# Reading bank Y on the scalar engine one product earlier, and reordering the first Strassen-like pair of each FFN

## The chip, the cores and the metric

One NeuronCore of a Trainium2 chip runs the whole kernel. The metric is the device time of one execution in microseconds. Three runs of the kernel before lie between 2317.99 and 2319.35 us, with a median of 2318.83 us. Engine names are those of the profile: PE (matrix multiply; its weight loads are PEld), DVE (vector), ACT (scalar), POOL (GpSimd) and SP (which issues the DMAs).

## What is computed

The reference is one encoder layer for 1280 tokens of width 1024 in float32: a SwiGLU half-step, a mixing step, and a second SwiGLU half-step. Only the FFNs matter here:

```python
def _swiglu(x, w_gate, w_up, w_down):
    return (jax.nn.silu(x @ w_gate) * (x @ w_up)) @ w_down

h = x + 0.5 * _swiglu(_rmsnorm(x, ffn1_norm), ffn1_w_gate, ffn1_w_up, ffn1_w_down)
...                                       # attention, retention, w_out
h = h + 0.5 * _swiglu(_rmsnorm(h, ffn2_norm), ffn2_w_gate, ffn2_w_up, ffn2_w_down)
return _rmsnorm(h, final_norm)
```

The FFN is 2816 wide, which is 22 blocks of 128 columns, taken two at a time as 11 pairs.

## The kernel before

**Precision.** Every float32 operand is split into a high half (an ACT cast, tiles `wh`, `xh`) and a low half (a DVE subtraction, `wl`, `xl`). A product is three matmuls: high by high, low by high, high by low. The page's names `pa` (a PSUM bank), `wh`, `wl`, `xh`, `xl` are these.

**FFN.** The 1280 tokens stand in three chunks: two of 512 columns and one of 256. Pair 0 of an FFN is multiplied directly (`direct`). Pairs 1 to 10 go through `seven_eighths`: the 1024 tokens of the two wide chunks are multiplied with seven products in place of eight (a Strassen-like scheme), once for gate and once for up (`product`, m = 0 and 1). The products carry numbers: 1, 2, 6, 7, 5, 4, 3, in this order, with 21 for a block that only the 256-column chunk needs. `seven` makes the weight factors (sums `s1` to `s4` on DVE, then the two halves of each). `combos` makes the activation factors of 6, 7, 5 and 4 on DVE. A product here is 12 matmuls of 128x512.

**Banks.** One `product` has five of the eight PSUM banks. X takes product 1, and later 6, 5 and 3 are added on top; Z takes product 2; Y takes product 7, and 4 is added on top. d1 and d2 hold the 256-column chunk, with 24 matmuls of 128x256 each. Outputs are read off between products: `o11` = X after 1 plus Z, `o21` = -X after 6, minus Y after 4. `o22` needs X after product 5 and Y after product 7:

```python
o22 = s2(name="o22")
nc.scalar.activation(o22, X, AF.Copy, scale=-1.0)
nc.vector.tensor_tensor(o22, o22, Y, op=ALU.subtract)
```

Product 4 is added on Y, so its first matmul waits until that DVE subtraction has read Y.

**Order.** `Weaver` records every instruction and then lists them for each engine by a planner with costs of its own, so that the program of an engine is a fixed list which the engine runs in order. All rows of the trace carry the line of `emit` (L433). Buffers of 128x512 come from one heap of 104 slots; a buffer gets a slot in the order in which the planner allocates.

**Before and after the FFN.** In `Lead`, the factors of the tokens are split; in the second FFN they come from the output projection (`out_unit`), whose last eight calls make chunk 2. Numbers at the end of a tile's name in the rows below only tell tiles apart.

Of the kernel before, what the change touches and what calls it, by code (L numbers as in the profile page):

```python
# [70 lines left out]
class Buf:  # L71
    def __init__(self, pool, shape, dt, tag, name, bufs, psum=False):
        self.args = (pool, shape, dt, tag, name, bufs)
        self.shape, self.tag, self.bufs, self.psum = shape, tag, bufs, psum
        self.width = shape[1]
        self.order = None
        self.left = 0
        self.end = 0.0
        self.accesses = []
        self.tile = None  # L80
# [19 lines left out]
class Weaver:  # L100
# [75 lines left out]
    def record(self, calls):  # L176
# [3 lines left out]
        for eng, method, a, k in calls:  # L180
            vals = [v for v in list(a) + list(k.values()) if isinstance(v, View)]
            outs = [k["out"]] if "out" in k else [a[0]]
            if k.get("accum_out") is not None:
                outs.append(k["accum_out"])
            outs = [v for v in outs if isinstance(v, View)]
            ins = [v for v in vals if not any(v is x for x in outs)]
            if method == "dma_start":
                v = (outs + ins)[0]
                nb = (v.box[1] - v.box[0]) * (v.box[3] - v.box[2]) * 4
                op.cost, op.lat, op.kind = 0.47, 2.0, nb  # L190
            else:
                op.cost += self.cost(eng, method, a, k, outs, ins)
                f = a[2] if method == "activation" and len(a) > 2 else None
                if f in (AF.Silu, AF.Exp):
                    op.kind = f
            for views, wr in ((ins, False), (outs, True)):
                for v in views:
                    b = v.buf
                    box = (0, P, 0, b.width) if b.psum else v.box
                    keep = []  # L200
                    for x in b.accesses:
                        (p0, p1, c0, c1), i, w = x

# [63 lines left out]
    def arrange(self, prio):  # L267
# [28 lines left out]
        self.peak = {n: max(t["seq"]) for n, t in self.tags.items()}  # L296

        def fresh(op):
            return [b for b in op.bufs.values() if b.tag is not None and not self.tags[b.tag]["done"][b.order]]

        def may(op):
            if op.eng == "SP" and op.idx > front() + self.AHEAD:
# [143 lines left out]
def tile_encoder_layer(ctx: ExitStack, tc: tile.TileContext, xT, wf1, w_in, w_out, wf2,  # L446
# [20 lines left out]
    def s2(dt=F32, name="t"):  # L467
        return nc.tile(hp, [P, 512], dt, "s2", nm(name), NS2)

    def two(W, name):  # L470

        if W <= 256:
            t = s2(F32R, name)
            return t[:, :W], t[:, 256:256 + W]
        return s2(F32R, name + "h"), s2(F32R, name + "l")

    def bank_a():
        return nc.tile(psp, [P, 512], F32, "p", nm("pa"), 8, True)
# [30 lines left out]
        nc.sync.dma_start(t, src)  # L509
        return t  # L510

    def halves(t, W=512):
        hi, lo = two(W, "w")
        split(t, hi, lo)
        return hi, lo

# [96 lines left out]
    def seven(r11, r12, r21, r22, W):  # L613
# [6 lines left out]
        yield 1, halves(r11, W)  # L620
        yield 2, halves(r12, W)
        nc.vector.tensor_tensor(s1, r21, r22, op=ALU.add)
        nc.vector.tensor_tensor(s2_, s1, r11, op=ALU.add)
        yield 6, halves(s2_, W)
        nc.vector.tensor_tensor(s3, r11, r21, op=ALU.add)
        yield 7, halves(s3, W)
        yield 5, halves(s1, W)
        yield 4, halves(r22, W)
        yield 21, halves(r21, W)
        nc.vector.tensor_tensor(s4, s2_, r12, op=ALU.add)  # L630
        yield 3, halves(s4, W)

    def norm_out(h, gcol, W, c0):
        pb = rms_rows(h, W)
        yield
        for kt in range(KT):
# [2 lines left out]
                                           op0=ALU.mult, op1=ALU.mult)  # L639
            nc.sync.dma_start(outT[:, kt, c0:c0 + W], t[:, :W])  # L640
            yield

    def ffn(tag, wsrc, leads, factors, load, after, direct_pairs):

# [7 lines left out]
        def product(t, m, hook):  # L652
# [49 lines left out]

        def direct(t, lead):

            ws, out, acts = {}, {}, {}

            def products(c):
                W = CH[c][1]
# [7 lines left out]
                for js in ((0, 1), (2, 3)) if c == 2 else ((0, 1, 2, 3),):  # L716
                    for k in range(2):
                        if k not in x:
                            x[k] = lead.x(c, k)
                        for j in js:  # L720
                            if (j, k) not in ws:
                                src = wsrc[t + j % 2 * HALF, :, j // 2, :]
                                ws[j, k] = halves(fetch(src[:, k * 512:(k + 1) * 512]))
                            part(out[c][j], ws[j, k], x[k], W, k == 0, k == 1)

            def close(c):
# [13 lines left out]
            close(1)  # L740
            return [acts[0][0], acts[1][0], acts[0][1], acts[1][1], *acts[2]]

        def seven_eighths(t, hook=lambda i: None):
            r = last.rows(2)
            acts = []
            for x in product(t, 0, lambda i: None):
                W = 512 if len(acts) < 4 else 256
                acts.append(gate(x, W, r if W < 512 else None))
            for i, x in enumerate(product(t, 1, hook)):
                W = 512 if i < 4 else 256  # L750
                up(acts[i], x, W, r if W < 512 else None)
            return acts
# [108 lines left out]
                first.update({j: [act(0, j)] for j in (1, 2, 6, 7, 5, 4, 3, 8, 9)})  # L861

        for t in range(direct_pairs, HALF):
            finish(t, seven_eighths(t, *[early] * (t == HALF - 1)))
        for c in range(3):
            h[c] = [None] * KT
        groups = [[0], [1, 2], [3, 4], [5, 6], [7, 8]]
# [54 lines left out]
    class Lead:  # L922


        def __init__(self, pairs, r2=None):
            self.pairs, self.r2 = pairs, r2

        def x(self, c, k):
            return self.pairs[c][4 * k:4 * k + 4]
# [7 lines left out]
    class First(Lead):  # L937


        def __init__(self):  # L940
            self.raw, self.pairs, self.r, self.n = {}, {0: [], 2: []}, {}, {}

        def x(self, c, k):
            if c != 1:
# [334 lines left out]
    for d in range(KT):  # L1279
        out_unit(1, d, cat[1])  # L1280
        if d == 3:
            cat[2] = cat_split(2)
    nx, xp = [], []
    for d in range(KT):
        out_unit(2, d, cat[2])
        if d in (0, 4):
# [11 lines left out]
        return t  # L1298

    def leads2():  # L1300
        yield Lead({0: xp[0], 1: xp[1], 2: x2})
        yield Lead({0: xp[0], 1: xp[1], 2: x2})

    def after2(c):
# [97 lines left out]
```

## Time and profile before

| | |
|---|---|
| median of 3 runs | 2318.83 us |
| the profiled execution, its own time | 2319.39 us |
| its span, first to last instruction | 2317.5 us |
| PE busy | 2270.6 us (98%) |
| DVE busy | 1589.7 us (69%) |
| ACT busy | 970.6 us (42%) |
| mean granted TensorE clock | 0.995 |

The span is 1.9 us shorter than the execution's time. PE is busy 98% of the span, and its idle time is the difference of 46.9 us. Which waits make it up stands in the view of waits; where they stand in time, in the timeline; what the clock did, in the view by windows. "pa <- DVE o" reads: a matmul into a bank `pa` was released by a DVE instruction that wrote `o`.

### The profile page before, as it was taken

What the parts mean: (1) busy time and instruction counts of PE and PEld (TensorE: products, weight loads), DVE (VectorE), ACT (ScalarE), POOL (GpSimd) and SP (SyncE); (2) the same over time, 40 slices, a digit from 0 to 9 for tenths busy, and PEclk for the clock granted to TensorE, in tenths of its full rate; (3) what the DMA queues carried; (4) which work ended last, traced back from release to release, by engine and by line L of the source; (5) the groups of instructions that cost most, each with busy time, mean ns of one, the idle gap of its engine ahead of it and who ended that gap; (6) DMA issues with size and microseconds to landing.
All of it is one profiled execution on the core that took longest, in us unless ns stands there. A gap on an engine that the chain in (4) does not pass through costs nothing.

```text
span 2317.5 us, 34127 instructions
## 1 busy us (share of the span) xinstructions
PE 2270.6 (98%) x12354; PEld 1937.2 (84%) x12354; DVE 1589.7 (69%) x3171; ACT 970.6 (42%) x2034; POOL 26.8 (1%) x31
## 2 busy tenths in 40 slices
PE   9999999999999999999999999989999999999998
PEld 8788888888888888887879979878888888888887
DVE  7966666556778876546778787666655555777866
ACT  7533443425422345234778474334333333432311
POOL 0000000000000000000000000000000000000000
PEclk9999999999999999999999999999999999999999
DMA  4333433345776643221134443234333334757722
GB/s 165 124 118 141 143 130 109 109 151 180 257 256 216 213 141 138 82 73 42 33 97 156 136 155 114 75 112 147 127 110 109 127 109 168 262 183 268 251 86 91
DMA packets 193417, 330.63 MB, mean 143 GB/s; under 512 B 20704, under 2 KB 45152, under 8 KB 193248
## 3 DMA queue, kind: packets, MB, share of 16 engines
q1 hardware_dynamic: 193248, 328.45, 41.0%
q8 instruction: 97, 1.59, 0.3%
q14 instruction: 72, 0.59, 0.1%
HBM read 226.65 MB, written 101.71 MB: 142 GB/s over the span
## 4 chain that ended last, share of the span: by engine, by line
PE 89%; DVE 5%; DMA 4%; issue 1%; ACT 1%; SPq 0%; POOL 0%; POOLq 0%; DVEq 0%; ACTq 0%
PE pa L433 63%; PE pb L433 25%; PE pc L433 2%; DMA raw<-wf 1%; DMA xa<-a 1%; DVE s L433 1%; DVE wl L433 1%; DVE h L433 1%; DMA h<-xT 1%; DVE o L433 1%; DVE xl L433 0%; DVE w L433 0%; DMA raw<-w_in 0%; DVE t L433 0%; SPq L433 0%
## 5 line engine op out<-in xcount | busy, mean ns | idle before, releaser
L433 PE MATMUL pa<-xh,wh 128*128 128x512 f32 x1664 | 659.9, 397 | 19.3 <-DVE o L433 15.3
L433 PE MATMUL pa<-xh,wl 128*128 128x512 f32 x1664 | 649.8, 390 | 8.0 <-DVE wl L433 8.0
L433 PE MATMUL pa<-xl,wh 128*128 128x512 f32 x1664 | 651.4, 391 | 1.0 <-DVE xl L433 1.0
L433 PE MATMUL pb<-xa,w 128*128 128x512 f32 (+1 forms) x2376 | 453.5, 352 | 6.0 <-ACT h L433 3.4
L433 PEld LDWEIGHTS pb<-xa,w 128*128 128x128 f32 x2376 | 386.4, 189 | 73.2 <-DVE h L433 6.3
L433 PEld LDWEIGHTS pa<-xh,wh 128*128 128x128 f32 x1664 | 314.0, 189 | 87.2 <-DVE o L433 19.1
L433 PEld LDWEIGHTS pa<-xh,wl 128*128 128x128 f32 x1664 | 313.5, 188 | 75.7 <-DVE wl L433 8.4
L433 PEld LDWEIGHTS pa<-xl,wh 128*128 128x128 f32 x1664 | 314.2, 189 | 58.7 <-DVE xl L433 1.8
L433 PE MATMUL pa<-x,wh 128*128 128x256 f32 x1824 | 337.5, 284 | 0.0
L433 PEld LDWEIGHTS pa<-x,wh 128*128 128x128 f32 x1824 | 294.9, 191 | 12.3
L433 DVE TENSOR_TENSOR wl<-raw,wh 128x512 fp32r<-128x512 f32 x372 | 244.4, 686 | 76.3 <-PE pa L433 38.6
L433 DVE SCALAR_TENSOR_TENSOR h<-pb,h 128x512 f32<-128x512 f32 (+1 forms) x360 | 223.4, 629 | 84.8 <-PE pb L433 81.9
L433 ACT CAST wh<-raw 128x512 fp32r<-128x512 f32 x372 | 217.2, 621 | 112.9 <-PE pa L433 49.8
L433 PE MATMUL pa<-x,wl 128*128 128x256 f32 x912 | 258.6, 284 | 0.1
L433 DVE TENSOR_TENSOR o<-o,pa 128x512 f32<-128x512 f32 x120 | 82.2, 685 | 179.6 <-PE pa L433 108.4
L433 ACT ACTIVATE o<-pa 128x512 f32<-128x512 f32 (+1 forms) x92 | 54.4, 591 | 312.6 <-PE pa L433 312.4
L433 PEld LDWEIGHTS pa<-x,wl 128*128 128x128 f32 x912 | 174.6, 191 | 0.4 <-DVE wl L433 0.3
L433 DVE TENSOR_TENSOR wl<-s,wh 128x512 fp32r<-128x512 f32 x160 | 106.9, 687 | 76.8 <-PE pa L433 64.0
L433 ACT CAST wh<-s 128x512 fp32r<-128x512 f32 x160 | 96.8, 619 | 34.4 <-PE pa L433 15.8
L433 ACT CAST w<-raw 128x256 fp32r<-128x256 f32 x144 | 53.7, 405 | 129.9 <-PE pb L433 97.8
L433 DVE TENSOR_TENSOR s<-s,raw 128x512 f32<-128x512 f32 (+1 forms) x152 | 85.2, 561 | 30.5 <-PE pa L433 28.5
L433 ACT CAST w<-s 128x256 fp32r<-128x256 f32 x144 | 56.0, 406 | 118.3 <-DVE s L433 68.1
(152 smaller groups left out, 2343.5 us busy)
## 6 DMA issues: line engine op xcount, KB each, us to landing
xa<-a SPq DMA_DIRECT2D x328, 256.0 KB, 5.1
raw<-wf SPq DMA_DIRECT2D x264, 256.0 KB, 4.3
a<-xh SPq DMA_DIRECT2D x142, 256.0 KB, 2.1
a<-xl SPq DMA_DIRECT2D x142, 256.0 KB, 3.3
raw<-w_in SPq DMA_DIRECT2D x132, 256.0 KB, 3.4
raw<-w_out SPq DMA_DIRECT2D x48, 256.0 KB, 3.1
a<-x SPq DMA_DIRECT2D x44, 256.0 KB, 2.5
h<-xT SPq DMA_DIRECT2D x32, 256.0 KB, 5.6
```

Of the source, the lines that this page charges most:

```text
L433: i = getattr(getattr(self.nc, eng), method)(*[r(x) for x in a], **{m: r(x) for m, x in k.items()})
```

## The change

Four things change.

- **Y is read first.** ACT reads Y as `o22` = -Y right after product 7, and DVE subtracts X after product 5. Product 4 may write to Y once ACT has read it, and product 3 may write to X once DVE has.
- **The first pair.** In the first pair that goes through `seven_eighths`, gate's products 1 and 2 are recorded, then up's products 1 and 2, then the rest of gate and the rest of up.
- **Slots.** In that pair the high and the low tile of a weight factor get their slots in one step (`mate`).
- **Weights ahead.** The eight weight blocks of the second FFN's pair 0 are fetched and split (`block`) ahead of the last eight calls of `out_unit`.

```diff
@@ Weaver.call
-                            b.order = len(t["bufs"])
-                            t["bufs"].append(b)
-                            op.allocs.append(b)
+                            for x in (b, b.mate) if b.mate is not None else (b,):
+                                x.order = len(t["bufs"])
+                                t["bufs"].append(x)
+                                op.allocs.append(x)
@@ two
-        return s2(F32R, name + "h"), s2(F32R, name + "l")
+        a, b = s2(F32R, name + "h"), s2(F32R, name + "l")
+        if together:
+            a.buf.mate, b.buf.mate = b.buf, a.buf
+        return a, b
@@ ffn
+    def block(wsrc, t, j, k):
+        return halves(fetch(wsrc[t + j % 2 * (NFF // 2), :, j // 2, k * 512:(k + 1) * 512]))
@@ product
-            for i, w in seven(*r, 512):
+            for i, w in seven(*r, 512, t == direct_pairs):
...
                 elif i == 7:
                     part(Y, w, xs[7], 512, True, True)
+                    o22 = s2(name="o22")
+                    nc.scalar.activation(o22, Y, AF.Copy, scale=-1.0)
                 elif i == 5:
                     part(X, w, xs[5], 512, False, True)
-                    o22 = s2(name="o22")
-                    nc.scalar.activation(o22, X, AF.Copy, scale=-1.0)
-                    nc.vector.tensor_tensor(o22, o22, Y, op=ALU.subtract)
+                    nc.vector.tensor_tensor(o22, o22, X, op=ALU.subtract)
...
                 hook(i)
-            return [o11, X, o21, o22, d1, d2]
+                if i == 2:
+                    yield
+            yield [o11, X, o21, o22, d1, d2]
@@ seven_eighths
-            for x in product(t, 0, lambda i: None):
+            ps = [product(t, 0, lambda i: None), product(t, 1, hook)]
+            next(ps[0])
+            if wait:
+                next(ps[1])
+            for x in next(ps[0]):
                 W = 512 if len(acts) < 4 else 256
                 acts.append(gate(x, W, r if W < 512 else None))
-            for i, x in enumerate(product(t, 1, hook)):
+            if not wait:
+                next(ps[1])
+            for i, x in enumerate(next(ps[1])):
@@ second FFN
+    ahead = {(j, k): block(wf2, 0, j, k) for j in range(4) for k in range(2)}
     for d in range(KT):
         out_unit(2, d, cat[2])
```

Three places of the engines' lists show what moves. The rows stand as each list has them, before and after apart.

PE in a pair of the second FFN, before: the last matmuls of d2 (`pa_3706`) and the first of product 4 on Y (`pa_3703`), which stands behind all of product 5's and 18 of d2's matmuls.

```order
L433 MATMUL pa_3706_17386<-x_3305_15321,wh_3726_16814 128x256 x2
L433 MATMUL pa_3706_17386<-x_3305_15321,wl_3727_17335 128x256 [waits DVE_49]
L433 MATMUL pa_3706_17386<-x_3307_15326,wh_3726_16814 128x256 x2
L433 MATMUL pa_3706_17386<-x_3307_15326,wl_3727_17335 128x256
L433 MATMUL pa_3703_17347<-xh_3390_15400,wh_3724_16808 128x512 [waits DVE_49]
L433 MATMUL pa_3703_17347<-xl_3391_15430,wh_3724_16808 128x512
```

After, product 4 on Y (`pa_3703`) follows product 5 on X (`pa_3702`) at once, and d2 comes behind it.

```order
L438 MATMUL pa_3702_17198<-xl_3425_15913,wh_3722_17270 128x512
L438 MATMUL pa_3702_17198<-xh_3424_15877,wl_3723_17312 128x512
L438 MATMUL pa_3703_17347<-xh_3390_15535,wh_3724_16808 128x512 [waits Activation_49]
L438 MATMUL pa_3703_17347<-xl_3391_15584,wh_3724_16808 128x512
L438 MATMUL pa_3703_17347<-xh_3390_15535,wl_3725_17333 128x512 [waits DVE_49]
```

Product 4's wait is now for ACT; all 24 matmuls of d2 stand behind product 4 and ahead of product 3.

DVE at the same place, before: five instructions, then the subtraction of Y from `o22`.

```order
L433 TENSOR_TENSOR wl_3763_17398<-raw_3739_16844,wh_3762_16974 128x512 [waits PE_49]
L433 TENSOR_TENSOR wl_3765_17400<-raw_3738_16827,wh_3764_16990 128x512 [waits PE_49]
L433 TENSOR_TENSOR s4_3748_17402<-s2_3746_17392,raw_3737_16819 128x512 [waits DVE_49]
L433 TENSOR_TENSOR wl_3802_17407<-raw_3788_17073,wh_3801_17272 128x512 [waits DVE_49]
L433 TENSOR_TENSOR o22_3723_17390<-o22_3723_17390,pa_3703_17347 128x512 [waits Activation_49]
```

After: the subtraction reads X (`pa_3702`), and the one of `o21` follows it.

```order
L438 TENSOR_TENSOR s3_3747_17377<-raw_3736_16769,raw_3738_16827 128x512
L438 TENSOR_TENSOR wl_3763_17384<-raw_3739_16844,wh_3762_16929 128x512 [waits PE_49]
L438 TENSOR_TENSOR wl_3755_17388<-s2_3746_17375,wh_3754_17379 128x512 [waits PE_49,Activation_49]
L438 TENSOR_TENSOR wl_3758_17401<-s3_3747_17377,wh_3757_17386 128x512 [waits Activation_49]
L438 TENSOR_TENSOR o22_3721_17369<-o22_3721_17369,pa_3702_17198 128x512 [waits PE_49]
L438 TENSOR_TENSOR o21_3718_17351<-o21_3718_17351,pa_3703_17347 128x512 [waits PE_49]
```

In each list some splits of the next factors stand ahead of the subtraction.

The second FFN's first pair on DVE, before: the low half of gate's plain factor 2 (`wl_3445`) stands behind the last combinations of the activations.

```order
L433 TENSOR_TENSOR xl_3421_15819<-n2_3417_15801,xh_3420_15809 128x512 [waits DMAHW3_49,Activation_49]
L433 TENSOR_TENSOR xl_3423_15823<-t3_3418_15807,xh_3422_15815 128x512 [waits DMAHW4_49,Activation_49]
L433 TENSOR_TENSOR xl_3425_15827<-t1_3416_15793,xh_3424_15803 128x512 [waits DMAHW5_49]
L433 TENSOR_TENSOR xl_3427_15831<-t4_3419_15813,xh_3426_15821 128x512 [waits Activation_49]
L433 TENSOR_TENSOR wl_3445_15833<-raw_3429_15115,wh_3444_15207 128x512 [waits DMAHW7_49]
```

After, it stands some sixty rows further ahead (row 2116 in place of 2179), together with that of up's factor 1 (`wl_3460`).

```order
L438 SCALAR_TENSOR_TENSOR n2_3381_15289<-t1_3380_15284,xn_3276_15164 128x512 [waits DVE_49]
L438 TENSOR_SCALAR r_3326_15300<-pb_3325_15293 128x2 [waits PE_49]
L438 TENSOR_TENSOR t3_3382_15302<-xn_3276_15164,xn_3272_15116 128x512
L438 SCALAR_TENSOR_TENSOR t4_3383_15310<-n2_3381_15289,xn_3213_14943 128x512 [waits DVE_49]
L438 TENSOR_TENSOR wl_3445_15315<-raw_3429_15118,wh_3444_15218 128x512 [waits DMAHW1_49]
L438 TENSOR_TENSOR wl_3460_15319<-raw_3446_15144,wh_3459_15222 128x512 [waits DMAHW4_49]
```

On PE the plain products of gate and of up and part of d2 now stand ahead of product 6 (`pa_3432` with `wh_3464`); these are the last rows ahead of it.

```order
L438 MATMUL pa_3454_15977<-x_3341_15391,wh_3492_15251 128x256 x2
L438 MATMUL pa_3454_15977<-x_3341_15391,wl_3493_15427 128x256
L438 MATMUL pa_3432_15706<-xh_3384_15304,wh_3464_15966 128x512 [waits Activation_49]
L438 MATMUL pa_3432_15706<-xl_3385_15510,wh_3464_15966 128x512
L438 MATMUL pa_3432_15706<-xh_3384_15304,wl_3465_15981 128x512 [waits DVE_49]
```

In the first FFN's first pair, PE before: product 6 (`pa_245`) and product 7 (`pa_246`) of the gate go one fourth at a time, as the activations come.

```order
L433 MATMUL pa_245_959<-xh_197_966,wh_259_517 128x512 [waits Activation_49]
L433 MATMUL pa_245_959<-xl_198_1066,wh_259_517 128x512 [waits DVE_49]
L433 MATMUL pa_245_959<-xh_197_966,wl_260_526 128x512
L433 MATMUL pa_246_1086<-xh_199_1061,wh_262_524 128x512 [waits Activation_49]
L433 MATMUL pa_246_1086<-xl_200_1073,wh_262_524 128x512 [waits DVE_49]
L433 MATMUL pa_246_1086<-xh_199_1061,wl_263_531 128x512
L433 MATMUL pa_285_1092<-xh_163_846,wh_295_606 128x512
```

After, up's product 6 (`pa_263`) takes part, and both plain products of up are done before.

```order
L438 MATMUL pa_245_987<-xh_197_992,wh_277_517 128x512 [waits Activation_49]
L438 MATMUL pa_245_987<-xl_198_1076,wh_277_517 128x512 [waits DVE_49]
L438 MATMUL pa_245_987<-xh_197_992,wl_278_526 128x512
L438 MATMUL pa_246_1119<-xh_199_1071,wh_280_524 128x512 [waits Activation_49]
L438 MATMUL pa_246_1119<-xl_200_1083,wh_280_524 128x512 [waits DVE_49]
L438 MATMUL pa_246_1119<-xh_199_1071,wl_281_531 128x512
L438 MATMUL pa_249_736<-x_11_128,wh_287_483 128x256 x2
L438 MATMUL pa_249_736<-x_11_128,wl_288_558 128x256
L438 MATMUL pa_263_1056<-xh_197_992,wh_297_581 128x512 [waits Activation_49]
L438 MATMUL pa_263_1056<-xl_198_1076,wh_297_581 128x512
```

The twelve matmuls of up's product 6 now stand among the fourths of gate's 6 and 7, three to each; up's product 2 (`pa_285`), which stood there before, has moved ahead of them, and three of d1's matmuls stand there in place of nine.

## Rows read from the trace of the kernel before

**Rows 1.** The page, part 1: busy time, share and instructions of each engine.

```profile
PE 2270.6 (98%) x12354; PEld 1937.2 (84%) x12354; DVE 1589.7 (69%) x3171; ACT 970.6 (42%) x2034; POOL 26.8 (1%) x31
```

**Rows 2.** The waits of PE, whole span: us in total, times, longest us.

```profile
PE pa L433 <- DVE o L433: 15.3, 17, 1.4
PE pa L433 <- DVE wl L433: 8.0, 1, 8.0
PE pa L433 <- ACT xh L433: 4.0, 2, 2.4
```

**Rows 3.** The waits of PE, 140 to 510 us (the first FFN).

```profile
PE pa L433 <- DVE o L433: 8.0, 8, 1.4
```

**Rows 4.** The waits of PE, 1525 to 2015 us (the second FFN).

```profile
PE pa L433 <- DVE o L433: 7.3, 9, 0.8
```

**Rows 5.** Timeline of PE, a pair of the second FFN: start, duration, instruction, [idle before].

```profile
1682.31 0.40 PE L433 MATMUL pa<-x,wh 128*128 128x256 f32 x2
1682.55 0.28 PE L433 MATMUL pa<-x,wl 128*128 128x256 f32 x1
1683.64 0.50 PE L433 MATMUL pa<-xh,wh 128*128 128x512 f32 x1 [0.81 <-DVE o L433]
1683.98 0.39 PE L433 MATMUL pa<-xl,wh 128*128 128x512 f32 x1
1684.21 0.40 PE L433 MATMUL pa<-xh,wl 128*128 128x512 f32 x1
```

**Rows 6.** Timeline of DVE around the same place.

```profile
1680.49 1.29 DVE L433 TENSOR_TENSOR wl<-raw,wh 128x512 fp32r<-128x512 f32 x2 [0.83 <-PE pa L433]
...
1682.91 0.68 DVE L433 TENSOR_TENSOR o<-o,pa 128x512 f32<-128x512 f32 x1
```

**Rows 7.** Timeline of DVE, a pair of the first FFN.

```profile
297.53 0.69 DVE L433 TENSOR_TENSOR wl<-raw,wh 128x512 fp32r<-128x512 f32 x1 [0.82 <-PE pa L433]
...
300.14 0.68 DVE L433 TENSOR_TENSOR o<-o,pa 128x512 f32<-128x512 f32 x1
```

**Rows 8.** Timeline of ACT, the same pair of the second FFN.

```profile
1680.72 0.60 ACT L433 ACTIVATE o<-pa 128x512 f32<-128x512 f32 x1 [3.08 <-PE pa L433]
1681.22 1.82 ACT L433 CAST wh<-s 128x512 fp32r<-128x512 f32 x3
```

**Rows 9.** Timeline of PE, where the casts of 1681.22 are first used.

```profile
1698.30 0.40 PE L433 MATMUL pa<-xh,wh 128*128 128x512 f32 x1
```

**Rows 10.** Windows: length, busy of PE, PEld, DVE, ACT, POOL, clock, DMA share, GB/s.

```profile
36.00:48.00 12.00, 12.00 (x71) 10.92 (x70) 7.43 (x16) 6.11 (x11) 2.99 (x3) 0.86 0.01 2
...
92.00:100.00 8.00, 3.32 (x10) 1.55 (x9) 7.93 (x14) 4.42 (x8) 0.00 (x0) 0.88 0.00 1
100.00:104.00 4.00, 3.64 (x9) 2.78 (x9) 4.00 (x9) 2.78 (x6) 0.00 (x0) 0.50 0.00 0
...
300.00:304.00 4.00, 3.12 (x15) 2.62 (x16) 1.04 (x3) 0.68 (x2) 0.00 (x0) 1.00 0.00 0
...
1506.00:1514.00 8.00, 0.27 (x2) 0.00 (x0) 7.97 (x14) 3.95 (x8) 0.00 (x0) 0.83 0.99 328
1514.00:1518.00 4.00, 3.74 (x9) 2.97 (x10) 2.80 (x6) 3.39 (x7) 0.00 (x0) 0.50 0.58 210
```

**Rows 11.** Timeline of PE, first pair of Strassen products in the second FFN.

```profile
1505.87 0.40 PE L433 MATMUL pa<-xl,wh 128*128 128x512 f32 x1
1514.26 0.80 PE L433 MATMUL pa<-xh,wl 128*128 128x512 f32 x1 [7.99 <-DVE wl L433]
```

**Rows 12.** Timeline of DVE, the same stretch.

```profile
1499.04 0.69 DVE L433 TENSOR_TENSOR s<-s,pa 128x512 f32<-128x512 f32 x1 [13.87 <-PE pa L433]
...
1513.52 0.68 DVE L433 TENSOR_TENSOR wl<-raw,wh 128x512 fp32r<-128x512 f32 x1
```

**Rows 13.** Timeline of PE, first pair of Strassen products in the first FFN.

```profile
94.36 0.49 PE L433 MATMUL pa<-xh,wh 128*128 128x512 f32 x1 [1.67 <-ACT xh L433]
...
99.30 0.80 PE L433 MATMUL pa<-xh,wh 128*128 128x512 f32 x1 [2.35 <-ACT xh L433]
```

More of the change, by code (lines that the diff above doesn't have):

```diff
@@ L75, in __init__ @@
         self.width = shape[1]
-        self.order = None
+        self.order = self.mate = None
         self.left = 0
@@ L298, in fresh @@
         def fresh(op):
-            return [b for b in op.bufs.values() if b.tag is not None and not self.tags[b.tag]["done"][b.order]]
+            new = [b for b in op.bufs.values() if b.tag is not None and not self.tags[b.tag]["done"][b.order]]
+            for b in list(new):
+                if b.mate is not None and not self.tags[b.tag]["done"][b.mate.order] and b.mate not in new:
+                    new.append(b.mate)
+            return new
         def may(op):
@@ L468, in s2, with two @@
         return nc.tile(hp, [P, 512], dt, "s2", nm(name), NS2)
-    def two(W, name):
+    def two(W, name, together=False):
         if W <= 256:
@@ L510, in fetch, with halves @@
         return t
-    def halves(t, W=512):
-        hi, lo = two(W, "w")
+    def halves(t, W=512, together=False):
+        hi, lo = two(W, "w", together)
         split(t, hi, lo)
@@ L611, in combos, with seven @@
         return {i: pair(t, 512) for i, t in ((6, n2), (7, t3), (5, t1), (4, t4))}
-    def seven(r11, r12, r21, r22, W):
+    def seven(r11, r12, r21, r22, W, together=False):
         if W > 256:
@@ L619, in seven @@
             s1, s2_, s3, s4 = a[:, :W], a[:, W:2 * W], b[:, :W], b[:, W:2 * W]
-        yield 1, halves(r11, W)
-        yield 2, halves(r12, W)
+        yield 1, halves(r11, W, together)
+        yield 2, halves(r12, W, together)
         nc.vector.tensor_tensor(s1, r21, r22, op=ALU.add)
         nc.vector.tensor_tensor(s2_, s1, r11, op=ALU.add)
-        yield 6, halves(s2_, W)
+        yield 6, halves(s2_, W, together)
         nc.vector.tensor_tensor(s3, r11, r21, op=ALU.add)
[L626 to L629, printed above, removed]
+        yield 7, halves(s3, W, together)
+        yield 5, halves(s1, W, together)
+        yield 4, halves(r22, W, together)
+        yield 21, halves(r21, W, together)
         nc.vector.tensor_tensor(s4, s2_, r12, op=ALU.add)
-        yield 3, halves(s4, W)
+        yield 3, halves(s4, W, together)
     def norm_out(h, gcol, W, c0):
@@ L703, in direct @@
         def direct(t, lead):
-            ws, out, acts = {}, {}, {}
+            ws, out, acts = lead.ws, {}, {}
             def products(c):
@@ L721, in products @@
                             if (j, k) not in ws:
-                                src = wsrc[t + j % 2 * HALF, :, j // 2, :]
-                                ws[j, k] = halves(fetch(src[:, k * 512:(k + 1) * 512]))
+                                ws[j, k] = block(wsrc, t, j, k)
                             part(out[c][j], ws[j, k], x[k], W, k == 0, k == 1)
@@ L741, in direct, with seven_eighths @@
             return [acts[0][0], acts[1][0], acts[0][1], acts[1][1], *acts[2]]
-        def seven_eighths(t, hook=lambda i: None):
+        def seven_eighths(t, wait, hook=lambda i: None):
             r = last.rows(2)
             acts = []
-            for x in product(t, 0, lambda i: None):
+            ps = [product(t, 0, lambda i: None), product(t, 1, hook)]
[3 more added lines that the diff above has]
+            for x in next(ps[0]):
                 W = 512 if len(acts) < 4 else 256
                 acts.append(gate(x, W, r if W < 512 else None))
-            for i, x in enumerate(product(t, 1, hook)):
+            if not wait:
+                next(ps[1])
+            for i, x in enumerate(next(ps[1])):
                 W = 512 if i < 4 else 256
@@ L863, in ffn @@
         for t in range(direct_pairs, HALF):
-            finish(t, seven_eighths(t, *[early] * (t == HALF - 1)))
+            finish(t, seven_eighths(t, t == direct_pairs, *[early] * (t == HALF - 1)))
         for c in range(3):
@@ L925, in __init__ @@
         def __init__(self, pairs, r2=None):
-            self.pairs, self.r2 = pairs, r2
+            self.pairs, self.r2, self.ws = pairs, r2, {}
         def x(self, c, k):
@@ L940, in __init__ @@
         def __init__(self):
-            self.raw, self.pairs, self.r, self.n = {}, {0: [], 2: []}, {}, {}
+            self.raw, self.pairs, self.r, self.n, self.ws = {}, {0: [], 2: []}, {}, {}, {}
         def x(self, c, k):
@@ L1300, in leads2 @@
     def leads2():
-        yield Lead({0: xp[0], 1: xp[1], 2: x2})
+        a = Lead({0: xp[0], 1: xp[1], 2: x2})
+        a.ws = ahead
+        yield a
         yield Lead({0: xp[0], 1: xp[1], 2: x2})
```

## The prediction

> **What bounds the kernel now.** I read the busy shares first: PE is busy 2270.6 us of a span of 2317.5 us, 98% [rows 1], so whatever shortens the time must take away PE's waits, or slow matmuls, and there are 46.9 us of waits. The view of waits comes next [rows 2]. It puts 15.3 us on DVE's `o` in 17 waits, 8.0 us on one wait for a `wl`, and 4.0 us on two waits for `xh`. The windowed waits split the first group: 8 waits with 8.0 us in the first FFN [rows 3], 9 with 7.3 us in the second [rows 4]. That is one for nearly every pair, so it is a pattern and not an accident. The windows then show two stretches in which PE is mostly idle, 92 to 100 us and 1506 to 1514 us, each followed by one with a granted clock of 0.50, the lower of the two levels (1.2 GHz) [rows 10]. The reader is to see that three places carry the change: the steady pairs and the first pair of each FFN.
>
> **Part A, reading Y early (steady pairs).** At 1680.49 product 5 has ended, which releases DVE; DVE then runs four other instructions and starts `o` at 1682.91 [rows 6]. PE meanwhile runs 18 matmuls of d2 and waits 0.81 us for `o` [rows 5]. The wait costs more than its idle time: 1682.55 to 1683.64 is 1.09 us where 0.12 is usual (two matmuls of 128x256 from 1682.31 to 1682.55), and the next step takes 0.34 us where 0.23 is usual [rows 5]. That is 0.97 + 0.11 = 1.08 us, 0.27 more than the idle 0.81. Over 17 waits: 15.3 + 17 x 0.27 = 19.9 us.
>
> After the change two waits stand in place of this one. Product 4 waits for ACT's read of Y, which can begin when product 7 ends; product 5 lies between, 12 x 0.23 = 2.8 us, and the read takes 0.60 us [rows 8]. ACT had been idle for 3.08 us ahead of its old read [rows 8], so it is free. Product 3 waits for DVE's subtraction of X. What lies between is product 4 and all of d2: 2.8 + 24 x 0.12 = 5.6 us. DVE needed 3.1 us in the second FFN (1680.49 to the end of `o`, 1683.59) [rows 6] and 3.3 us in the first (297.53 to 300.82) [rows 7], and the new list has no more instructions ahead of the subtraction than the old one. So 2.3 us are left over, and all 19.9 us should go. Bounds: 0 (the wait only moves to product 3) and 19.9; I take 19.9, since the margin is over twice what one DVE instruction takes (0.68).
>
> **Part B, the second FFN's first pair.** PE stands from 1505.87 to 1514.26, a step of 8.39 us where 0.23 is usual: 8.2 us [rows 11]. What it waits for is the low half of a weight, which DVE runs at 1513.52, after 22 instructions that began at 1499.04 [rows 12]; DVE had idled 13.87 us right before that [rows 12]. The new list puts this split sixty rows further ahead, into a stretch in which DVE has time. Behind the wait 9 matmuls take 3.74 us at clock 0.50 [rows 10], 0.42 each against 0.23, so 1.7 us, and some 0.3 until the clock is back: 2.0 us. Together 10.2 us.
>
> What is late next is product 6. Its low half now has 34 instructions ahead of it, counted from the one at 1499.04. At the old rate, 14.48 us for 22 [rows 12], of which 0.60 each is steady and 1.2 us is gaps, it starts at 1499.04 + 34 x 0.60 + 1.2 = 1520.7 and ends at 1521.4. PE has, from 1505.6 - 2.8 - 1.4 = 1501.4, four plain products (11.0 us), both d1 (48 x 0.12 = 5.8 us) and 33 matmuls of d2 (4.0 us) until 1522.2, and asks for the low half 0.5 us later. The margin is 1.3 us. Bounds of B: 3 (a new wait of 5 us, with the clock down again) and 10.2; I take 9.9.
>
> The eight splits ahead of the output projection add no work, they move it: DVE's 8 x 0.60 = 4.8 us fit in the 13.87 us of idle time. Their loads move ahead of others in SP's queue, and at the 328 GB/s of [rows 10] a block of 256 KB takes 0.8 us, 6.4 us for eight. If PE had to wait for all of that it would be 6.4 us lost; I take 0, since no wait of PE for a DMA is among the large ones [rows 2].
>
> **Part C, the first FFN's first pair.** From 92 to 100 us DVE is busy 7.93 of 8 us and PE 3.32 [rows 10]: DVE's combinations set the pace, PE waits 1.67 and 2.35 us for their casts [rows 13]. The 4.7 us idle and the 9 matmuls in 4 us at clock 0.50 that follow (1.9 us lost) [rows 10], with some 0.5 us until the clock is back, make 7 us in all. The change doesn't make DVE's list of combinations shorter. It gives PE more to do between them: three matmuls of up's product 6 with each fourth, and less of d1. By the first wait that is six more of 0.23 and six fewer of 0.12, 0.7 us; by the second three more, 0.7 us. So the waits shrink by 1.4 us. Against this, eight weight instructions move into 36 to 48 us, where DVE is busy 7.43 of 12 us [rows 10]: 8 x 0.60 = 4.8 us into 4.6 us of idle time. They nearly fit; if they hold up the norm behind them, up to 2 us are lost. Bounds of C: -2 and 7.
>
> The clock fell after these waits, and did not fall in 300 to 304 us after a wait of 1.4 us [rows 3, 10]. Since two waits stay, I give it three chances in four to fall again. C is 1.4 us then and 1.4 + 2.4 = 3.8 us otherwise; I take 2.0.
> The Trainium skill ("TensorE: Matmul & The Clock Gate", section "HAM oscillation — how this bites in real kernels") says that a wait lets the clock fall and the next burst starts cold, and its section on a second failure mode that many short waits do it too. The trace agrees at 100 us and not at 300 us. By the rule C would be 1.4 us, and 3.8 us if it did not hold.
>
> **The sum.** 19.9 + 9.9 + 2.0 = 31.8 us. From the profiled execution's 2319.39 us that leaves 2287.6 us. The median of the runs is 0.56 us lower than the profiled one, which gives 2287.0; I say 2287.5, with half a microsecond for small new waits.
>
> **Rivals.**
> *Waits return in the first pairs.* The high half of product 6 is cast on ACT behind seven casts of newly loaded blocks, and the DMA engines are 0.99 busy from 1506 to 1514 [rows 10]. If those land late, B is 3 and C is 0 or less: 19.9 + 3 = 23 us, 2296 us. For it speaks the margin of 1.3 us, against it that PE's view of waits shows nothing large on a late cast of a weight in the old kernel, whose loads were as dense [rows 2].
>
> *The steady wait only moves.* If DVE reaches the subtraction of X more than 2.3 us later than it did `o`, product 3 waits in place of product 4, at the same price: A is 0, the time 2319.4 - 12 = 2307 us. Against it stands the list, where only splits whose inputs are early come first.
>
> *ACT blocks, and it gets slower.* ACT's read of Y waits at the head of its list, and the casts behind it wait with it; in the old trace the three casts start at 1681.22, when the read of X is done [rows 8]. If PE came to wait for such a cast in each product, the read and one cast would lie on its path, 0.60 + 0.62 = 1.22 us, in 2 x 20 products: 49 us, 2336 us. It decides from 0.9 us each on, where it eats the gain. Against it: PE first uses those casts at 1698.30 [rows 9], 17 us after they start.
> The Trainium skill ("PSUM — Partial Sum Buffer", section "Engine vs sequencer instructions") says that the queues of ScalarE and VectorE are strict FIFO, which is the rule behind this rival. The trace agrees with it: nothing passes ACT's wait of 3.08 us.
>
> *The change doesn't do what it says.* If the planner's other moves cost what the three places bring, the time stays at 2318.8 us.
>
> **How the numbers follow.** Forecast 0.66, with its own range of 2282 to 2293 us (37 us if C brings all 7, and 26 us if B and C fall short by 6); waits in the first pairs 0.17; the wait moves 0.08; no change 0.05; ACT blocks 0.04. All bounds at their best give 19.9 + 10.2 + 7 = 37.1 us, 2281.7 us for the median. From 2281 to 2303 us the range holds the first two cases and leaves out the rest, about 0.18. A difference of 0.2%, 4.6 us, is about what a measurement of this kernel can tell from none. Faster by more: 0.66 + 0.17 + 0.08 = 0.91; within it 0.05; slower 0.04.
>
> **What would show it.** Right: no wait of PE for DVE's `o` between 140 and 510 us or between 1525 and 2015 us, and pairs about 1.1 us apart from before in the second FFN; no 8 us wait for `wl` and a clock of 1.0 around 1514 us; two waits for `xh` near 94 and 99 us that are each about 0.7 us shorter. Wrong: waits of product 3 for `o` (17 of them, up to 1.4 us), a wait for `wl` or `wh` of product 6 after the plain products, or ACT's casts among the releasers of PE.

## The result and the profile after

The changed kernel takes 2286.31 us (median of 4 runs, 2284.04 to 2288.26), the kernel before 2319.09 (2317.99 to 2320.01) on the same chip: a ratio of 0.9858, 95% interval 0.9841 to 0.9876. Forecast was 2287.5, range 2281 to 2303. The profiled execution took 2286.97 us, its span is 2285.0. The page, part 1, against [rows 1]:

```profile
PE 2263.6 (99%) x12354; PEld 1936.0 (85%) x12354; DVE 1596.3 (70%) x3171; ACT 974.3 (43%) x2034; POOL 26.8 (1%) x31
```

The waits of PE over the whole span (us in total, times, longest), against [rows 2]:

```profile
PE pb L438 <- DVE h L438: 3.1, 5, 1.4
PE pb L438 <- DVE sq L438: 1.9, 1, 1.9
PE pb L438 <- DVE r L438: 1.7, 1, 1.7
PE pa L438 <- ACT xh L438: 1.6, 2, 1.0
```

The 15.3 us for DVE's `o` and the 8.0 us for `wl` are gone. Between 140 and 510 us no wait is listed at all [rows 3]; between 1525 and 2015 us, in place of [rows 4], only this one:

```profile
PE pb L438 <- DVE h L438: 0.8, 1, 0.8
```

The timeline of PE in a steady pair of the second FFN (start, duration, instruction), against [rows 5]: the last matmul of product 5 and the first of product 4, then the last of d2 and the first of product 3.

```profile
1655.51 0.39 PE L438 MATMUL pa<-xh,wl 128*128 128x512 f32 x1
1655.74 0.39 PE L438 MATMUL pa<-xh,wh 128*128 128x512 f32 x1
...
1661.21 0.28 PE L438 MATMUL pa<-x,wl 128*128 128x256 f32 x1
1661.33 0.40 PE L438 MATMUL pa<-xh,wh 128*128 128x512 f32 x1
```

DVE there, against [rows 6], and ACT, against [rows 8]:

```profile
1655.78 1.29 DVE L438 TENSOR_TENSOR wl<-s,wh 128x512 fp32r<-128x512 f32 x2 [1.29 <-PE pa L438]
1656.99 0.68 DVE L438 TENSOR_TENSOR o<-o,pa 128x512 f32<-128x512 f32 x1
```

```profile
1653.27 0.60 ACT L438 ACTIVATE o<-pa 128x512 f32<-128x512 f32 x1 [1.66 <-issue]
```

Both steps are the usual 0.23 and 0.12 us. ACT's read of Y ends at 1653.87, 1.87 us before product 4; DVE's subtraction of X ends at 1657.67, 3.66 us before product 3. So both new waits have their events early.

The windows answer to [rows 10] (length, busy of PE, PEld, DVE, ACT, POOL, clock, DMA share, GB/s):

```profile
36.00:48.00 12.00, 10.32 (x55) 9.22 (x54) 10.91 (x22) 6.38 (x11) 3.16 (x3) 0.88 0.01 1
92.00:100.00 8.00, 6.31 (x28) 4.70 (x27) 7.97 (x14) 4.42 (x8) 0.00 (x0) 0.98 0.18 65
100.00:104.00 4.00, 3.06 (x7) 1.54 (x5) 3.96 (x8) 2.44 (x4) 0.00 (x0) 0.50 0.42 131
300.00:304.00 4.00, 4.00 (x21) 3.37 (x20) 1.34 (x3) 2.06 (x4) 0.00 (x0) 1.00 0.00 0
1506.00:1514.00 8.00, 8.00 (x56) 7.43 (x56) 6.25 (x11) 5.03 (x10) 0.00 (x0) 1.00 0.09 35
1514.00:1518.00 4.00, 4.00 (x19) 3.31 (x18) 3.15 (x6) 2.39 (x6) 0.00 (x0) 1.00 0.02 4
```

In the second FFN's first pair PE is busy throughout, at clock 1.00. In the first FFN's first pair the hole and the low clock remain: PE's waits there, against [rows 13]:

```profile
97.90 0.49 PE L438 MATMUL pa<-xh,wh 128*128 128x512 f32 x1 [1.03 <-ACT xh L438]
...
102.84 0.80 PE L438 MATMUL pa<-xh,wh 128*128 128x512 f32 x1 [0.57 <-ACT xh L438]
```

They come 3.5 us later than before (94.36, 99.30). The reason stands in DVE's timeline of after: the weight splits that moved ahead keep the norm waiting.

```profile
43.41 1.28 DVE L438 TENSOR_TENSOR wl<-s,wh 128x512 fp32r<-128x512 f32 x2
44.61 0.15 DVE L438 TENSOR_SCALAR r<-pb 128x2 f32<-128x2 f32 x1
...
51.14 1.41 DVE L438 SCALAR_TENSOR_TENSOR xn<-h,par,pb 128x512 f32<-128x512 f32 x2 [1.23 <-PE pb L438]
```

PE waits 1.68 us for that `r`:

```profile
44.82 1.60 PE L438 MATMUL pb<-ones,sq 128*128 128x1 f32 x8 [1.68 <-DVE r L438]
```

In the kernel before, DVE wrote the same `r` at 41.59 and was at `xn` at 47.60:

```profile
41.59 0.16 DVE L433 TENSOR_SCALAR r<-pb 128x2 f32<-128x2 f32 x1 [0.92 <-PE pb L433]
...
47.60 2.06 DVE L433 SCALAR_TENSOR_TENSOR xn<-h,par,pb 128x512 f32<-128x512 f32 x3 [0.94 <-PE pb L433]
```

The clock has a part in it too. Over 40 to 56 us the granted clock (the last figure but two of a windows row) is 0.89 before and 0.79 after; a value between 0.50 and 1.00 is a mean over a window in which the clock changed its level.

```profile
40.00:56.00 16.00, 15.20 (x110) 14.63 (x109) 12.05 (x24) 10.60 (x20) 2.99 (x3) 0.89 0.00 1
40.00:56.00 16.00, 14.32 (x90) 13.92 (x89) 13.50 (x27) 8.73 (x17) 3.23 (x3) 0.79 0.00 0
```

**Where the time came from.** I compare start times at equal numbers of matmul columns done; the difference is the gain so far, good to about 0.1 us. Times are those of before.

| up to | gain so far | in this stretch |
|---|---|---|
| 140 us (start, first pair) | -0.25 | -0.25 |
| 510 us (first FFN, steady) | 10.20 | 10.45 |
| 1490 us | 11.41 | 1.21 |
| 1520 us (second FFN, first pair) | 21.41 | 10.00 |
| 2015 us (steady) | 31.58 | 10.17 |
| 2300 us | 32.58 | 1.00 |

### The profile page after: what moved, and what is told of

It reads as the page before. It is cut to its first block, busy times and chain, and to the rows that moved or that the text cites. A ratio compares the mean times of both kernels' runs of the same rounds, so it can differ in the third digit from the quotient of the medians.

```text
span 2285.0 us, 34157 instructions
## 1 busy us (share of the span) xinstructions
PE 2263.6 (99%) x12354; PEld 1936.0 (85%) x12354; DVE 1596.3 (70%) x3171; ACT 974.3 (43%) x2034; POOL 26.8 (1%) x31
## 4 chain that ended last, share of the span: by engine, by line
PE 92%; DMA 4%; DVE 2%; issue 1%; ACT 1%; SPq 0%; POOL 0%; POOLq 0%; DVEq 0%; ACTq 0%
PE pa L438 64%; PE pb L438 27%; DMA raw<-wf 2%; PE pc L438 2%; DMA xa<-a 1%; DMA h<-xT 1%; ACT sq L438 0%; DMA raw<-w_in 0%; DVE xl L438 0%; DVE t L438 0%; DVE wl L438 0%; DVE s L438 0%; DMA h<-hf 0%; DMA a<-xh 0%; DMA a<-xl 0%
## 5 line engine op out<-in xcount | busy, mean ns | idle before, releaser
L438 PEld LDWEIGHTS pa<-x,wh 128*128 128x128 f32 x1824 | 293.0, 192 | 10.1 <-ACT wh L438 0.9
L438 DVE TENSOR_TENSOR s<-raw,raw 128x512 f32<-128x512 f32 (+1 forms) x116 | 70.1, 604 | 53.0 <-PE pa L438 42.8
L438 ACT ACTIVATE sq<-h 128x512 f32<-128x512 f32 (+1 forms) x96 | 51.1, 557 | 126.4 <-DVE h L438 124.6
```

Of the source, the lines that this page charges most:

```text
L438: i = getattr(getattr(self.nc, eng), method)(*[r(x) for x in a], **{m: r(x) for m, x in k.items()})
```

## Experiments

Gains are taken in the same way, against the profile of before.

**1. Only the early reading of Y.** The kernel before with this:

```diff
                 elif i == 7:
                     part(Y, w, xs[7], 512, True, True)
+                    o22 = s2(name="o22")
+                    nc.scalar.activation(o22, Y, AF.Copy, scale=-1.0)
...
-                    nc.vector.tensor_tensor(o22, o22, Y, op=ALU.subtract)
+                    nc.vector.tensor_tensor(o22, o22, X, op=ALU.subtract)
```

> The kernel before with one change: ACT reads Y (o22 = -Y) after product 7 and DVE subtracts X after product 5. Theory (the three places add up: 21 us in the steady pairs, 10 us in the second FFN's first pair, nothing net in the first FFN's): 2319 - 20.5 = 2298.5 us, between 2297 and 2300; no wait of PE for DVE's o between 140 and 510 or 1525 and 2015 us; the 8 us wait for wl in the second FFN stays. Rival (early reading of Y only pays together with the other parts, or the list of the first pairs moves with it): 2303 us or more, or 2295 or less. Rival (the wait moves to product 3): waits for o in the steady pairs, about 2319 us.

Measured: 2296.63 us, just under the expected 2297 to 2300; ratio 0.9903 (0.9886 to 0.9919). No wait for `o` is left; the wait for `wl` stays, as PE's waits between 1480 and 1535 us show:

```profile
PE pa L433 <- DVE wl L433: 8.0, 1, 8.0
```

It gains 10.4 us from 140 to 540, 10.1 from 1520 to 2015, and nothing from 1490 to 1520. So this edit is the steady gain, and none of the first pair's.

**2. All but the early reading.** The changed kernel with the old reading of X and Y.

```diff
-                    o22 = s2(name="o22")
-                    nc.scalar.activation(o22, Y, AF.Copy, scale=-1.0)
...
-                    nc.vector.tensor_tensor(o22, o22, X, op=ALU.subtract)
+                    nc.scalar.activation(o22, X, AF.Copy, scale=-1.0)
+                    nc.vector.tensor_tensor(o22, o22, Y, op=ALU.subtract)
```

> The changed kernel with the old reading of X and Y (X on ACT after product 5, then Y on DVE); all else as changed. Theory (the parts add up: 20.9 us belong to the early reading): 2286 + 21 = 2307, with 15 to 17 waits for DVE's o of 15 us in all back, and no 8 us wait for wl. Rival (the new first pairs also shift the planner's lists, so that the waits in the steady pairs are gone or halved by themselves): 2286 to 2297, under 8 us of waits for o.

Measured: 2309.64 us, ratio 0.9962 (0.9947 to 0.9976). Over the whole span:

```profile
PE pa L438 <- DVE o L438: 14.0, 16, 1.4
PE pb L438 <- DVE h L438: 3.2, 4, 1.1
PE pa L438 <- DVE wl L438: 3.0, 4, 2.3
```

The waits for `o` are back, and 10.0 us are gained from 1490 to 1520. Of 13.4 us gained by 1920 us, 2.9 are lost again by 2015, where the planner's list differs and a new wait of 2.3 us for `wl` stands. The rival (waits halved by themselves) is out. Experiments 1 and 2 save 22.5 and 8.7 us against 33 for all, so the parts nearly add up.

**3. Slots not taken together.** `together` left at False in `seven`.

```diff
-            for i, w in seven(*r, 512, t == direct_pairs):
+            for i, w in seven(*r, 512):
```

> The changed kernel, but high and low slots of the weight factors are not taken in one step; the list of the first FFN's first pair stays that of the changed kernel. Theory (the slots taken together bring the second FFN's 10 us, since without them the low half of gate's factor 2 stands behind all combinations again, at row 2179 of DVE's list): one wait of 6 to 8 us for wl near 1475 to 1495 us, clock 0.50 behind it, 2296 us, between 2294 and 2297.5. Rival (recording the plain factors of gate and up first is what brings it): 2286 to 2288 us.

Measured: 2299.15 us, ratio 0.9917 (0.9902 to 0.9932), which is above the expected 2294 to 2297.5. The wait is back, later and longer than expected:

```profile
1502.43 0.80 PE L438 MATMUL pa<-xh,wl 128*128 128x512 f32 x1 [8.55 <-DVE wl L438]
```

In DVE's list `wl_3445` stands at row 2179 again, where the kernel before has it, though the recording order is the new one. The clock is 0.50 for the whole of 1498 to 1508 us, and 11.5 us are lost against the changed kernel from 1490 to 1520.

**4. Gate recorded whole, then up.** Slots still together.

```diff
-            finish(t, seven_eighths(t, t == direct_pairs, *[early] * (t == HALF - 1)))
+            finish(t, seven_eighths(t, False, *[early] * (t == HALF - 1)))
```

> The changed kernel, but gate and up of the first pair are recorded one after the other, as before; slots are still taken together. Theory (slots taken together suffice, since the planner by itself puts up's plain products ahead of gate's product 6 in the second FFN): no wait above 2 us in the second FFN's first pair, 2286 to 2288 us; in the first FFN the normalised tiles xn start near 47.6 us again in place of 51.1, and PE's two waits for xh near 94 and 99 us are 1.7 and 2.4 us again, so that the first FFN's first pair comes out the same within 1 us. Rival (the recording order brings the 10 us): product 6 waits 5 to 11 us for its factor, 2293 to 2299 us. Forecast's part C (the recording order is worth 2 us in the first FFN): 2288 to 2289 us.

Measured: 2290.61 us (2286.12 to 2292.93), ratio 0.9876 (0.9859 to 0.9892): above the expected 2286 to 2288 and below the rival's 2293, with an interval that overlaps that of the changed kernel. No wait is listed between 1480 and 1535 us, and 10.0 us are gained there. The planner puts up's plain products ahead of product 6 by itself. The profile is that of the fastest run, so what the three slower ones lost is in no trace. What the recording order is worth, 0 to 4 us, stays unclear here; experiment 7, which leaves it out as well, is as fast as the changed kernel.

**5. Nothing fetched ahead.**

```diff
-    ahead = {(j, k): block(wf2, 0, j, k) for j in range(4) for k in range(2)}
...
-        a.ws = ahead
```

> The changed kernel without the eight weight blocks of the second FFN's pair 0 fetched and split ahead of the last output projection. Theory (they only move work that was hidden before as well): 2286 us within 1.5 us, the second FFN's first pair without a wait above 1 us. Rival (they free the time in which the low halves of the plain factors are split): a wait of 2 to 8 us for wl or wh between 1475 and 1515 us, 2289 to 2297 us.

Measured: 2284.70 us, ratio 0.9851 (0.9834 to 0.9867), 10.0 us gained from 1490 to 1520. The fetching ahead is worth nothing here.

**6. First FFN's first pair as before.** Slots together and the new order in the second FFN alone.

```diff
-            for i, w in seven(*r, 512, t == direct_pairs):
+            for i, w in seven(*r, 512, tag == 2 and t == direct_pairs):
...
-            finish(t, seven_eighths(t, t == direct_pairs, *[early] * (t == HALF - 1)))
+            finish(t, seven_eighths(t, tag == 2 and t == direct_pairs, *[early] * (t == HALF - 1)))
```

> The changed kernel, but the first FFN's first pair as before (no order of factors, no slots taken together there); the second FFN's first pair and the reading of Y as changed. Theory (the first FFN's part nets nothing, since the eight weight instructions that now stand ahead hold up the norm by 3.5 us, which eats what the shorter waits give): 2286.3 us within 1.2 us; xn starts near 47.6 us; waits for xh of 1.7 and 2.4 us. Forecast's part C: 2288.3 us or more. Rival (the first FFN's part costs): 2284 us or less.

Measured: 2285.34 us, ratio 0.9856 (0.9841 to 0.9871). The waits for `xh` are 1.83 and 2.34 us again, and the time is no longer than with the edit. The intervals overlap, so a part of C's 2 us could still hide in them.

**7. Two edits only, beside the changed kernel.** Early reading, and slots together in the second FFN's first pair: the edits of 4 and 5 and the first line of 6, in one kernel. The changed kernel ran again on the same chip.

> Only two of the edits: Y read early in every pair, and the slots of a high and a low half taken together in the second FFN's first pair. Factors recorded gate first, then up; nothing fetched ahead; the first FFN's first pair as before. Theory (only these two edits carry the gain, 20.9 + 10.0 us, and the rest nets to nothing): 2319 - 31 = 2288, within 3 us of the changed kernel on the same chip; no wait over 2 us between 1480 and 1530 us; waits of 1.7 and 2.4 us for xh near 94 and 99 us. Rival (the order of recording or the fetching ahead is needed once the other is gone too): the 8 us wait for wl comes back, 2297 to 2299.

> The changed kernel again, to stand beside the version with two edits on the same chip. Theory: 2286 (2284 to 2288), and 0 to 3 us from the version with two edits; rival (the four edits together are worth more than two): 4 us or more ahead of it.

Measured: 2286.02 us (2283.44 to 2286.98), ratio 0.9858 (0.9843 to 0.9873), and the changed kernel 2285.18 us (2284.19 to 2287.60), ratio 0.9858 (0.9843 to 0.9872). The same. Two edits carry all that can be timed; no version beats the changed kernel by a measurable amount.

**8. Extra reads of X on DVE.** Five, then eight, right behind the subtraction, in each of the 40 products; product 3 must wait for them.

```diff
                     nc.vector.tensor_tensor(o22, o22, X, op=ALU.subtract)
+                    for _ in range(5):
+                        nc.vector.tensor_tensor(s2(name="again"), o22, X, op=ALU.add)
```

> The changed kernel with five more DVE additions that read bank X (into tiles that nothing uses) right behind o22 -= X in each of the 40 gate and up products, so that product 3 must wait for them too. They hold X 5 x 0.60 = 3.0 us longer. Theory (what the changed kernel's trace shows: X is free 3.7 us before product 3 starts): no wait of PE for them in the steady pairs, the time within 4 us of 2286. Rival (the forecast's margin of 2.3 us): PE waits 0.7 us in each product, 40 x (0.7 + 0.27) = 39 us, 2325 us. Rival (DVE becomes the bound by its 40 x 5 x 0.6 = 120 us more): waits of PE for wl and xl in place of waits for the added reads.

> The same with eight more reads of X, 4.8 us. Theory (cover 5.6 us, of which 1.95 us are used): product 3 waits 1.1 us in each of the steady products, with 0.27 us more that its idle time does not show, 40 x 1.4 = 55 us, 2341 us; the waits are for the added reads and nothing else large. Rival (the planner or DVE's idle time hides them): under 2300 us. Rival (DVE as a whole becomes the bound): over 2360 us with waits for wl and xl.

Measured, one run each: 2321.67 and 2332.54 us. With five, DVE rises from 61.59 to 71.44 us of 100 in the second FFN's steady pairs, and PE stays full there:

```profile
1600.00:1700.00 100.00, 100.00 (x532) 86.33 (x531) 71.44 (x118) 41.43 (x74) 0.00 (x0) 1.00 0.36 127
```

No wait for `again` is listed anywhere, with the same 5.6 us of matmuls ahead of product 3 in 33 of 40 products. In a steady pair the five reads end at 1605.82, and product 3 starts 1.52 us later:

```profile
1602.74 3.08 DVE L438 TENSOR_TENSOR again<-o,pa 128x512 f32<-128x512 f32 x5
1607.34 0.40 PE L438 MATMUL pa<-xh,wh 128*128 128x512 f32 x1
```

So the margin is over 3.0 us and the forecast's 2.3 is too small. The time missed the expected 2286 by 35 us and came near the first rival's 2325, but not by its mechanism: the time is lost to later weights and `h`, much as the second rival has it. Seven of the eight waits for `wh`, 8.0 us, stand in the first FFN between 140 and 510 us. PE's waits, five reads:

```profile
PE pa L438 <- ACT wh L438: 9.4, 8, 2.2
PE pa L438 <- DVE wl L438: 6.7, 14, 2.5
PE pb L438 <- ACT h L438: 5.1, 1, 5.1
```

With eight, the expected wait in each product did not come; there are three:

```profile
PE pa L438 <- DVE again L438: 2.0, 3, 1.3
```

The planner now lists PE's matmuls of many of these products in another order, so this size doesn't measure the margin. A busier DVE does cost a lot, most of it around the last pairs of each FFN: with eight reads 20 us between 480 and 560 and 17 between 1900 and 2050, with five 7 and 13.

**9. An improvement tried: one combination of the first FFN's first pair on POOL,** on top of 6, with POOL's cost in the planner set for it.

```diff
-        nc.vector.tensor_tensor(t3, b22, b12, op=ALU.subtract)
+        (nc.gpsimd if spare else nc.vector).tensor_tensor(t3, b22, b12, op=ALU.subtract)
```

> The version in which only the second FFN's first pair is changed, and in addition one of the four combinations of activations (t3 = b22 - b12) of each column block runs on POOL in place of DVE, in both FFNs' first pairs. Theory (DVE's combinations set the pace of the first FFN's first pair, 4.8 us for a fourth, now 4.2): the wait for xh near 94 us goes, the one near 99 us falls from 2.4 to under 1.5 us, together 2 to 3 us, 2281 to 2283.5 us; less if the clock falls all the same. Rival (POOL and DVE get in each other's way, or POOL is too slow): DVE's instructions in 60 to 100 us take longer than 0.68 us, 2285 us or more.

Measured: 2290.86 us, ratio 0.9872 (0.9858 to 0.9887): slower than 6 by 5.5 us of the medians and 3.7 us by the ratios, whose intervals overlap. It is no gain. POOL's group, by form (busy, mean ns, idle before):

```profile
L438 POOL TENSOR_TENSOR t<-xn,xn 128x512 f32<-128x512 f32 x8 | 11.9, 1523 | 13.1 <-DVE xn L438 7.5 <-DMA raw<-wf 5.6
```

1.52 us where DVE takes 0.68. The profile, that of the slowest run (2292.95 us), shows the rival (POOL and DVE get in each other's way), outside the 60 to 100 us in which it was looked for. POOL's subtractions run from 53.29 to 59.24 us, and DVE's eight splits beside them take 2.9 us longer than in 6, more than the four instructions of 0.60 us that POOL takes off DVE. The three splits that start while POOL runs take 1.36 to 1.78 us each, the other five 0.68. First 6, then this run:

```profile
54.28 4.90 DVE L438 TENSOR_TENSOR xl<-xn,xh 128x512 fp32r<-128x512 f32 x8
55.04 7.76 DVE L438 TENSOR_TENSOR xl<-xn,xh 128x512 fp32r<-128x512 f32 x8
```

In the second FFN the same happens, 7.86 against 4.90 us, again while POOL runs. DVE then comes late to `sq` there:

```profile
1444.56 0.89 PE L438 MATMUL pb<-ones,sq 128*128 128x1 f32 x4 [1.93 <-DVE sq L438]
```

Of the 8.6 us by which this profile ends behind that of 6, 5.4 are lost from 1440 to 1460 us, where the clock falls as well (0.58 and 0.56 in 1444 to 1448 and 1448 to 1452), and 2.3 by 140 us. In the first FFN's first pair a wait of 2.41 us for `xh` stays, at 101.60, and one of 1.42 us for `xl`, at 97.77, is new.

## Why the prediction was right, step by step

**A, 19.9 us: right.** Measured 10.45 + 10.17 = 20.6, and experiment 1 has it from that edit alone. The step that turned idle time into price (0.27 us more than the idle 0.81) is needed: the listed 15.3 us alone would be 5 short. The margin of product 3 was mis-sized, 3.66 us against 2.3 in the pair shown, and 2.8 to 4.6 us in the 36 of 40 products that have product 4 and d2 in this order: I took DVE's old delay, with four instructions ahead of the subtraction (four it is in [rows 6] and in the list ahead of the prediction, not five), where two stand now. With either there is no wait, so it did not matter.

**B, 9.9 us: right.** Measured 10.0, again in experiments 2, 4, 5 and 6. Which edit does it, the prediction left open: experiment 3 shows that it is the slots. With slots taken one by one, the split of the low half stood late in the list; that it stood there because its slot was given late is what the edit was built on, and no run tests it by itself. The margin at product 6 was thinner than the forecast 1.3 us. DVE's low half:

```profile
1510.07 1.29 DVE L438 TENSOR_TENSOR wl<-s,wh 128x512 fp32r<-128x512 f32 x2
```

The first of the two is product 6's; with 0.68 each it ends at 1510.75, and PE asks for it 0.45 us later:

```profile
1511.20 0.39 PE L438 MATMUL pa<-xh,wl 128*128 128x512 f32 x1
```

The 34 instructions ahead of it, from 1487.63 on, took 22.4 us in place of the forecast 21.6, since DVE's gaps among them were longer than the assumed 1.2 us. The cost of 0 for the loads ahead agrees with experiment 5.

**C, 2.0 us: the size is open, two of its steps were off.** Of ten profiles, five have the new recording order there and five the old, with this gain so far (us) and this granted clock (the number of the experiment behind each):

| list, run | 92 us | 104 us | 140 us | clock 96-100, 100-104 |
|---|---|---|---|---|
| new, changed kernel | -2.82 | 1.19 | -0.25 | 0.97, 0.50 |
| new, again (7) | -1.68 | 2.32 | 2.08 | 0.75, 0.82 |
| new, 5 | -0.90 | 3.10 | 2.83 | 0.69, 0.88 |
| new, 3 | -2.35 | 1.53 | 1.36 | 1.00, 1.00 |
| new, 2 | -1.08 | 2.94 | 2.37 | 1.00, 1.00 |
| old, before | 0 | 0 | 0 | 0.76, 0.50 |
| old, 1 | 0.18 | 0.46 | 1.05 | 1.00, 0.58 |
| old, 6 | 0.18 | 0.21 | 0.87 | 1.00, 0.58 |
| old, 4 | 0.66 | 0.83 | 1.51 | 1.00, 0.57 |
| old, two edits (7) | -0.53 | -0.82 | -0.96 | 0.58, 0.50 |

The means at 140 us are 1.7 and 0.5, a difference of 1.2 with a scatter of about 1 in each group; the times (6 and 7) can't tell it from 0.

The step that failed is "they nearly fit": at 92 us the new list is 1.9 us behind (means -1.8 and 0.1). PE waits 1.2 to 2.2 us for `r` in all five profiles with the new list and in none with the old one, and DVE starts `xn` 1.6 to 3.5 us later than in the kernel before. Not all of the 1.9 us is that wait, since the clock from 40 to 56 us differs too: it is 0.79 or 0.89 with the new list, 0.89 or 1.00 with the old one. In the profiles with 0.89 alone, three new and two old, the means at 92 us are -1.2 and -0.3, about 1 us apart.

The other step, the shorter waits, has the right size where the clock holds: in experiment 2's profile, at 1.00 throughout, the two waits for `xh` are 1.04 and 1.66 us, 0.63 and 0.69 shorter than before, against 0.7 each. From 92 to 140 us the new list gains 3.4 to 3.8 us in four profiles, against 3.8 forecast without a fall of the clock, and 2.6 in the changed kernel's, where the clock is at 0.50 longest; the 1.4 forecast for that case was too small. From 92 to 104 us the gain is 3.9 to 4.0 us in all five, with the clock at 0.50 and at 1.00 alike, which fits DVE setting the pace: where the clock falls, PE's waits for `xh` and `xl` are shorter (2.6 us in the changed kernel's profile, 4.0 in experiment 2's). That reading is argued from these two profiles, not tested by itself.

The rest, about 2 us, was not in the sum: PE's wait for `h` ahead of 600.38 us fell from 2.4 to 0.8, and one of 0.86 us for `h` at 2023.68 is gone, which gained 1.1. The first was 1.7 us when the same program ran again, so part of it is scatter. That the total came within 1.2 us of the forecast is partly luck: in this profile C brought 2.2 us less than forecast, and these 2 us made up for it. Of the rivals, none came: no wait moved to product 3, and the longest wait for one of ACT's casts is 1.0 us.

## What to carry to other kernels

When two banks must be read into one result, read the one that is needed again first on the engine that is idle, and let the later product's end carry the other read; then check the margin for each bank by itself. Where a scheduler gives slots in its own order, a wait for half of an operand can be a slot given late: look for a split whose inputs were long there. Work that moves ahead "into idle time" needs a look at what stands right behind it in that engine's list, since a mean of idle time over 12 us hid a delay of 1.6 to 3.5 us here. And before work goes to an idle engine, compare how long the same instructions of the busy one take with and without it: here eight took 7.8 us in place of 4.9.

## What was not expected of the hardware

The clock behind the same order of work is not the same each time. The new list has 0.50 from 100 to 104 us in one profile, 0.82 and 0.88 in two, and 1.00 in two, after waits of the same size. In the changed kernel's profile waits of 1.03 and 0.66 us, before 97.90 and 99.06, are followed by 0.50; in experiment 2's these are followed by 1.00, and so is a longer one:

```profile
96.16 0.50 PE L438 MATMUL pa<-xh,wh 128*128 128x512 f32 x1 [1.04 <-ACT xh L438]
97.32 0.50 PE L438 MATMUL pa<-xl,wh 128*128 128x512 f32 x1 [0.66 <-DVE xl L438]
101.10 0.50 PE L438 MATMUL pa<-xh,wh 128*128 128x512 f32 x1 [1.66 <-ACT xh L438]
```

The Trainium skill ("TensorE: Matmul & The Clock Gate", section "HAM oscillation — how this bites in real kernels") has the burst after a wait start cold, in a kernel whose waits are for DMA and longer than these. The five profiles with the old order agree (0.50 to 0.58), and two of the five with the new one do not (1.00 from 96 to 104 us). So one profile can't price the clock's part of a stretch with waits of 1 to 2 us.
